# A scheduled hybrid layer kernel: context keys in the first job, later input norms, earlier input sums, fewer attention bank turns

## The chip, the cores and the metric

The kernel runs on one core of a Trainium2 chip. The metric is device time in microseconds (us) from the start to the end of one execution; a median of several executions is given. The core has five engines with their own instruction queues: TensorE (PE) multiplies and transposes, VectorE (DVE), ScalarE (ACT) and GpSimd (POOL) work elementwise, and SyncE (SP) issues the transfers here. Each engine has its instructions in one list, in the order in which they run; one whose operands aren't there waits, and those behind it with it.

## The reference, cut to what matters

One layer on 1024 latent tokens and 256 context tokens of width 1024, all in float32:

```python
mod_x = silu(c) @ w_ada + b_ada;  mod_c = silu(c_ctx) @ w_ada + b_ada     # shift, scale, gate
pl = split((rms_norm(x)   * (1 + sc_x) + sh_x) @ w_in)                      # 11 parts
pc = split((rms_norm(ctx) * (1 + sc_c) + sh_c) @ w_in)
# branch A: gated linear attention, 4 heads, key width 128, value width 256, chunks of 64, both directions
la = log_sigmoid(lowrank @ w_decay + b_decay) / 16
o_gla = forward scan + backward scan, each started from the context's final state
# branch B: differential attention, 8 heads, two score maps of width 64, value width 128
q1, q2, k1, k2 = rope(rms_norm(.) * gain);  keys: context and latent, 1280
a = softmax(q1 k1' / 8) - lam * softmax(q2 k2' / 8);  o_diff = a @ v
y = sigmoid(m_gla)  * ((rms_norm(o_gla)  * gain * silu(gla_gate))  @ w_br_gla) \
  + sigmoid(m_diff) * ((rms_norm(o_diff) * gain * silu(diff_gate)) @ w_br_diff)
return x + g_x * (y @ w_out)
```

The parts of the projection are named by what they feed: GK and GQ (keys and queries of branch A), GV, GG (its values and gate), DK, DQ, DV, DG (branch B), and MG, MD (the merge gates, "m").

## The kernel before, in words

**Precision.** A float32 product is made of three matmuls: each operand is split in a high part (ACT copies it, rounding) and a low part (DVE or POOL subtracts), and `mm3` adds high-high, low-high and high-low. So every weight tile and every activation costs a copy on ACT and a subtraction on DVE or POOL ("split") before PE can use it.

**Order.** The program is written by generators ("tasks") that run on the host while it is built. A class `Driver` keeps a clock for each engine with estimated costs, and lets that task go on whose operands are there first; so tasks of different stages interleave, and the order in which instructions are emitted is the order in each engine's queue. PE's clock is the Driver's time. `On(t, "ACT")` waits until ACT has come near t, `AtPE` until PE has, `Event` until another task has set it; `prio` breaks ties. Buffers are taken with `acq(tag)` and given back with `rel`; their numbers stand in the table `TAGS` ("w" has 16, "p" 5, "pl" 4, "e5" 6, "b1" 2). A table that ACT must load for another function has no cost in the Driver. Since every elementwise instruction is issued by one helper, all of them have line L190 in the profile, all matmuls L329, all transposes L355, all transfers L294; tiles are told apart by name.

**Stages.** (1) `prologue`: two passes of the modulation's matrix-vector product (`ada(0)`: shift and scale, `ada(1)`: the rest; PE gs, go <- w, cs and copies p<-gs), the norms of ten tiles of 128 tokens (`xnorm`: a square with its sum on ACT, a power on POOL, a multiplication on DVE), their transposes (tp <- ident, g) and the modulated, split input tiles h (`hblock`). A small job makes the low-rank decays (`prep_lr`; its la tiles are g, made by exp and log on ACT). (2) Plain projections, a list `first` of seven jobs: GK and GQ for the latent tokens, GK for the context, then dk and m by halves. A job streams its raw weights (raw), splits them (w <- raw) and walks through its items; an item is one tile of 128 output channels by up to 512 tokens, or the other way about. (3) From about 177 us branch A's scans (glab, glaf), its decayed keys and queries (ge, gqe, gqr, gkk) and their transposes and scores (gt, go, gs) run beside the later jobs. (4) From about 441 us the four large projections GV, DV, GG, DG by seven products in place of eight (`sums7`, `raws7`): sums of input blocks and of weight blocks first, s1 to s4 for the input, then the products. The sums of inputs go through p tiles; s2 overwrites input tiles h. (5) Branch A's chunks, to about 1005 us. (6) Attention: 64 units of one head and 128 queries. A unit has score banks for both maps, 1280 keys each: four banks' worth in two tiles of 128x1024, and a tail of 2 x 256 keys in one bank. `att_max` reduces a bank on DVE (sm <- s), a min joins main and tail, `att_exp` makes e with its sum on ACT, a combination of both maps follows on DVE (e <- e,sm,e), `att_tr` transposes e by groups of 4, 4 and 2 key tiles into a bank b1 for which there are two buffers, ACT copies it (ac), POOL splits it (at), and `att_av` multiplies with vv for a pair of units (b). `att_fin` normalises the pair's result (b1k), transposes it back and stores it (d_bT). Where PE has room, "fills" run: products of branch A's output with its projection (mb, mc <- h, wt), which are also what is left for behind attention. (7) The last products to 1748 us.

The parts that the change touches are these functions as they stand before:

## Time and profile before

| | |
|---|---|
| median of 3 runs | 1751.24 us (1751.02 to 1751.32) |
| the profiled execution | 1749.87 us, of which its span is 1748.2 us |
| mean granted PE clock | 0.978 of full |
| busy: PE, DVE, POOL, ACT | 1654.4, 1170.5, 951.4, 816.7 us |
| projections and branch A, 0 to 1005 us; score phase, 1004.7 to 1531.2 us | PE stands 27.0 us of the latter's 526.5 |

A row of a time line gives the start and length in us, the engine, the line, the operation, out <- in, and in square brackets how long the engine stood before it and what ended that. A row of a group gives the count, the busy time, the mean in ns and the idle time before. In a table of stretches each engine has its busy time and number of instructions; then come the granted clock, the DMA engines' busy share and GB/s. The granted clock is PE's, as a share of full.

### The profile page before, as it was taken

How to read it: one execution, taken by the hardware profiler on the slowest of the kernel's cores; microseconds unless marked ns; L12 is line 12 of the kernel's file. 1: busy time of each engine (PE TensorE's matmuls, PEld its weight loads, DVE VectorE, ACT ScalarE, POOL GpSimd, SP SyncE). 2: the span in 40 equal slices, each digit the busy share in tenths (PEclk: the TensorE clock that was granted, in tenths of full speed). 3: DMA queues.
4: the chain of work that ended last, by engine and by line, in shares of the span. 5: the costliest groups of instructions: out<-in, count | busy, mean ns of one | idle time of the engine just before them, and what ended most of it. 6: DMA issues, size and time to landing. Idle time of an engine off the chain costs nothing. (4 is left out here: it accounts for less than half of the span.)

```text
span 1748.2 us, 25274 instructions
## 1 busy us (share of the span) xinstructions
PE 1654.4 (95%) x8381; PEld 1365.3 (78%) x8381; DVE 1170.5 (67%) x1902; ACT 816.7 (47%) x1662; POOL 951.4 (54%) x1018
## 2 busy tenths in 40 slices
PE   8799799999889999999999798999999999998999
PEld 3578687888768888888888587888887788787887
DVE  4673986882844456757676568877787787735694
ACT  4675655642333334443233356565665555531241
POOL 1501775673633245655565548687788887880000
PEclk9899899999999999999999899999999999999999
DMA  8546566444225374457999823543774535368431
GB/s 301 187 151 215 165 200 202 149 135 142 84 85 161 117 253 154 160 181 250 301 297 309 225 81 102 148 123 103 216 235 129 153 103 149 94 208 296 144 105 72
DMA packets 273491, 300.82 MB, mean 172 GB/s; under 512 B 24488, under 2 KB 195408, under 8 KB 273360
## 3 DMA queue, kind: packets, MB, share of 16 engines
q1 hardware_dynamic: 273360, 299.20, 55.0%
q8 instruction: 66, 1.08, 0.3%
q14 instruction: 65, 0.53, 0.1%
HBM read 198.99 MB, written 100.14 MB: 171 GB/s over the span
## 5 line engine op out<-in xcount | busy, mean ns | idle before, releaser
L190 POOL TENSOR_TENSOR at<-ac,at 128x512 fp32r<-128x512 f32 (+1 forms) x192 | 238.1, 1240 | 16.0
L190 DVE TENSOR_REDUCE sm<-s 128x1 f32<-128x1024 f32 (+1 forms) x192 | 195.0, 1039 | 45.9 <-PE s L329 43.7
L329 PE MATMUL mm<-w,h 128*128 128x512 f32 x864 | 218.4, 402 | 4.9 <-DVE us L190 4.9
L190 ACT ACTIVATE e<-s,sm 128x1280 f32<-128x1280 f32 x128 | 169.8, 1331 | 49.6 <-DVE sm L190 41.9
L190 POOL TENSOR_SCALAR at<-ac 128x512 fp32r<-128x512 f32 (+1 forms) x192 | 141.0, 735 | 94.9 <-ACT ac L190 92.2
L329 PEld LDWEIGHTS mm<-w,h 128*128 128x128 f32 x864 | 162.4, 191 | 38.3 <-DVE us L190 5.3
L329 PE MATMUL s<-kk,aq 128*128 128x512 f32 (+1 forms) x768 | 180.7, 369 | 10.9 <-ACT e L190 6.7
L329 PE MATMUL mb<-h,wt 128*128 128x512 f32 x696 | 189.6, 405 | 0.9 <-ACT ft L190 0.7
L190 ACT ACTIVATE ac<-b 128x512 f32<-128x512 f32 (+1 forms) x212 | 106.1, 506 | 146.9 <-PE b L355 110.3
L329 PEld LDWEIGHTS s<-kk,aq 128*128 128x128 f32 x768 | 122.5, 192 | 32.8 <-ACT e L190 16.2
L329 PEld LDWEIGHTS mb<-h,wt 128*128 128x128 f32 x696 | 122.7, 189 | 22.1 <-ACT ft L190 1.1
L329 PE MATMUL mm<-h,w 128*128 128x512 f32 x552 | 137.7, 399 | 1.2 <-POOL w L190 0.6
L329 PE MATMUL b<-at,vv 128*128 128x256 f32 x960 | 129.1, 283 | 4.4 <-ACT ac L190 2.4
L190 DVE TENSOR_TENSOR w<-raw,w 128x512 fp32r<-128x512 f32 x89 | 83.3, 956 | 69.1 <-ACT w L190 49.3
L329 PEld LDWEIGHTS b<-at,vv 128*128 128x128 f32 x960 | 119.7, 188 | 10.0 <-ACT ac L190 4.4
L329 PEld LDWEIGHTS mm<-h,w 128*128 128x128 f32 x552 | 103.9, 191 | 24.2 <-DVE w L190 1.3
L190 POOL TENSOR_TENSOR w<-raw,w 128x512 fp32r<-128x512 f32 x31 | 42.8, 1382 | 136.5 <-ACT w L190 98.1
L190 DVE SCALAR_TENSOR_TENSOR e<-e,sm,e 128x1280 f32<-128x1280 f32 x64 | 113.5, 1773 | 0.7
L329 PE MATMUL mc<-h,wt 128*128 128x512 f32 x456 | 109.4, 398 | 4.4 <-DMA h<-d_bT 3.9
L190 POOL TENSOR_TENSOR sm<-sm,nhalf 128x2 f32<-128x2 f32 (+2 forms) x94 | 104.0, 1106 | 12.9 <-DVE sm L190 7.5
L329 PEld LDWEIGHTS mc<-h,wt 128*128 128x128 f32 x456 | 85.5, 190 | 24.2 <-DMA h<-d_bT 5.2
L329 PE MATMUL ma<-w,h 128*128 128x512 f32 x384 | 101.3, 404 | 0.5 <-DVE gp L190 0.4
(372 smaller groups left out, 3393.9 us busy)
## 6 DMA issues: line engine op xcount, KB each, us to landing
raw<-in_w_in SPq DMA_DIRECT2D x44, 512.0 KB, 4.7
rb<-in_w_in SPq DMA_DIRECT2D x64, 256.0 KB, 2.9
aq<-d_qT SPq DMA_DIRECT2D x128, 128.0 KB, 3.2
d_kT<-pl SPq DMA_DIRECT2D x40, 256.0 KB, 2.4
d_dv<-pl SPq DMA_DIRECT2D x40, 256.0 KB, 2.6
kk<-d_kT SPq DMA_DIRECT2D x32, 320.0 KB, 5.1
gv<-d_v SPq DMA_DIRECT2D x40, 256.0 KB, 4.6
vv<-d_dv SPq DMA_DIRECT2D x16, 640.0 KB, 6.6
```

Source lines behind the costliest of these rows:

```text
L190: self.ins = f(out, *args, **kw).ins
L329: self.ins = self.nc.tensor.matmul(out, lhsT, rhs, start=start, stop=stop, skip_group_check=more).ins
```

## The change

Four things are changed, and each moves work of several engines, since the Driver makes the whole order anew.

*Prologue.* The norms of tiles 4 to 9 wait for an event that is set when both passes of the modulation have been copied out. The low-rank job's preparation waits for the second pass's shifts and scales, no longer for the last load of the plain jobs' weights. On ACT's queue, where the modulation's copy p<-gs (4x512) stood behind a weight split of another raw tile and two squares with their sums (g to p, sm), this stands before:

```order
L190 ACTIVATE w_556<-raw_505 128x512
L190 ACTIVATE w_560<-raw_505 128x512
L190 ACTIVATE w_576<-raw_526 128x512
L190 ACTIVATE w_580<-raw_526 128x512
L190 ACTIVATE p_548,sm_549<-g_115_540 128x1024
L190 ACTIVATE p_550,sm_551<-g_116_542 128x1024
L190 ACTIVATE p_590<-gs_331 4x512
L190 ACTIVATE p_552,sm_553<-g_117_544 128x1024
```

and this now:

```order
L190 ACTIVATE w_552<-raw_509 128x512
L190 ACTIVATE w_556<-raw_509 128x512
L190 ACTIVATE p_564<-gs_335 4x512
L190 ACTIVATE p_569,sm_570<-g_115_544 128x1024
L190 ACTIVATE w_593<-raw_530 128x512
L190 ACTIVATE p_571,sm_572<-g_116_546 128x1024
L190 ACTIVATE p_609<-tp_599,shsc_197 128x512
L190 ACTIVATE w_614<-raw_530 128x512
```

The copy has moved ahead of the second raw tile's splits and of all squares.

*Keys of the context.* They are further items of the first job: GK [0, 1, 2], 12 items instead of 8 in the first job and 4 in a third. The list `first` has six jobs, four loads of raw weights and eight splits are left out. ACT's queue now has this where the GK job ends (p_1363 and p_1365 are the copies of its last, context items) and GQ's weights (w<-raw) begin; g is the decays' la:

```order
L190 ACTIVATE w_1323<-raw_577 128x512
L190 ACTIVATE w_1333<-raw_648 128x512
L190 ACTIVATE w_1343<-raw_648 128x512
L190 ACT_TABLE_LOAD
L190 ACTIVATE g_255_1191<-g_255_1191 128x1280
L190 ACTIVATE g_264_1261<-g_264_1261 128x1280
L190 ACT_TABLE_LOAD
L190 ACTIVATE g_255_1191<-g_255_1191 128x1280
L190 ACTIVATE g_264_1261<-g_264_1261 128x1280
L190 ACTIVATE p_1363<-mm_1276 128x256
L190 ACTIVATE p_1365<-ma_1277 128x256
L190 ACTIVATE w_1385<-raw_1346 128x512
```

Three more splits, from w_1291 on, stand right ahead of these rows: six of GQ's eight weight splits are ahead of the decays' two table loads, the others behind them. On PE the first transpose of branch A (gt<-ident,ge) stood right at the end of the context job; it now stands 48 matmuls into the job dk0.

*Input sums.* `sums7` no longer waits for the end of the plain projections. The sum for s2, whose place is still read by these, is stored in DRAM (four tiles of 256 KB), and after them loaded again and split into the input tiles.

*Attention.* The min is issued in `att_max`, directly behind the reductions that it joins; the task for exp then waits for ACT only. The last groups of 2 key tiles of both queries of a pair share one bank (128x512), so a pair turns the bank seven times, not nine; the e buffers of both are kept until then. `att_ot` copies a pair's result out, and `att_fin` runs once for two pairs, on 128x512. On DVE's queue one unit had this before, in the middle of attention (sm<-s is a reduction, 128x1 of a map's 1024 keys, 128x2 of the tails; sm<-sm,sm a min; e<-e,sm,e the combination of the unit before):

```order
L190 TENSOR_REDUCE sm_12442<-s_1983_9410 128x1
L190 RECIPROCAL sm_12492<-sm_12262 128x1
L190 TENSOR_SCALAR sm_12492<-sm_12492,sm_12262,nlam 128x1
L190 TENSOR_REDUCE sm_12441<-s_1983_9410 128x2
L190 TENSOR_SCALAR sm_12442<-sm_12442,sm_12441 128x1
L190 TENSOR_REDUCE sm_12443<-s_1983_9410 128x1
L190 TENSOR_TENSOR b1k_12401<-b_2678_12418,b1k_12401 128x256
L190 TENSOR_SCALAR sm_12443<-sm_12443,sm_12441 128x1
L190 SCALAR_TENSOR_TENSOR e_2681_12430<-e_2682_12431,sm_12492,e_2681_12430 128x1280
```

and has this now:

```order
L190 TENSOR_REDUCE sm_12001<-s_1967_9386 128x1
L190 TENSOR_REDUCE sm_12000<-s_1967_9386 128x2
L190 TENSOR_SCALAR sm_12001<-sm_12001,sm_12000 128x1
L190 SCALAR_TENSOR_TENSOR e_2543_12015<-e_2549_12046,sm_12064,e_2543_12015 128x1280
L190 TENSOR_REDUCE sm_12002<-s_1967_9386 128x1
L190 TENSOR_SCALAR sm_12002<-sm_12002,sm_12000 128x1
```

Nothing stands between a min and the reduction that it needs. Between the first and the last score matmul PE's list has 672 fill matmuls before and 558 now; behind the last transposes of the final norm it has 597 of their kind before and 723 now.

The diff, without the build's lists of scratch tensors and the event handling that only serves these edits:

```diff
-        e5=("sbB", 6), at4=("sbB", 6), at2=("sbB", 2), ac=("sbB", 2), b1k=("sbB", 5), fin=(None, 2),
+        e5=("sbB", 6), at4=("sbB", 6), at2=("sbB", 2), ac=("sbB", 2), b1k=("sbB", 5), ot=("sbB", 3), fin=(None, 2),
...
+            if i > 3:
+                yield ev_md
...
+            else:
+                d.set(ev_md)
...
-        first = [tra(C_GK, [0, 1], self.post_gk), tra(C_GQ, [0, 1], self.post_gq), tra(C_GK, [2], self.post_gk),
+        first = [tra(C_GK, [0, 1, 2], self.post_gk), tra(C_GQ, [0, 1], self.post_gq),
...
-        yield self.ev_plain
         for k in range(4):
             yield from self.acq("p", 4)
             v = {}
@@ -950,16 +956,27 @@
             yield d.when(v["22"])
             self.either(v["11"], v["22"], v["11"], ALU.subtract)
             yield d.when(v["11"], v["12"])
+            self.store([(self.d_s2[k], v["11"])], ev=ev_s2[k])
             self.either(v["12"], v["12"], v["11"], ALU.subtract)
-            for o, y in (("s2", "11"), ("s1", "22"), ("s4", "12"), ("s3", "21")):
+            for o, y in (("s1", "22"), ("s4", "12"), ("s3", "21")):
                 yield d.when(v[y])
-                if o != "s2":
-                    self.op7[o, k] = [self.t("s7", [P, 512], F32R) for _ in range(2)]
-                hi, lo = self.op7[o, k]
+                hi, lo = self.op7[o, k] = [self.t("s7", [P, 512], F32R) for _ in range(2)]
                 self.act.activation(hi, v[y], AF.Copy)
                 e = self.either(lo, v[y], hi.bitcast(F32), ALU.subtract)
                 d.set(self.ev_op[o, k], e)
-            self.rel("p", e, 4)
+            yield ev_s2[k]
+            self.rel("p", max(e, ev_s2[k].t), 4)
+        yield self.ev_plain
+        for k in range(4):
+            yield from self.acq("p")
+            v = self.t("p", [P, 512])
+            self.dma(v, self.d_s2[k])
+            yield d.when(v)
+            hi, lo = self.op7["s2", k]
+            self.act.activation(hi, v, AF.Copy)
+            e = self.either(lo, v, hi.bitcast(F32), ALU.subtract)
+            d.set(self.ev_op["s2", k], e)
+            self.rel("p", e)
...
-        yield self.ev_wc
+        yield self.ev_sh[1]
...
-                    d.spawn(self.att_max(u["ev"][comp], u["mx"][comp], pm, 3 * comp, 3 * comp + 1), On(e, "DVE"), prio=-3)
+                    d.spawn(self.att_max(u, comp, s5, pm, 3 * comp, 3 * comp + 1), On(e, "DVE"), prio=-3)
...
-                    d.spawn(self.att_exp(u, comp, s5), On(e, "DVE"), prio=-3)
...
-    def att_max(self, ev, mx, pm, *banks):
+    def att_max(self, u, x, s5, pm, *banks):
+
+        mx = u["mt"] if x == 2 else u["mx"][x]
         self.dve.tensor_reduce(mx, pm, AX.X, ALU.max, negate=True)
         self.banked(self.dve.ins, "DVE", *banks)
-        self.d.set(ev)
+        self.d.set(u["ev"][x])
+        for c in range(2):
+            if u["ev"][2].t is not None and u["ev"][c].t is not None and c not in u["min"]:
+                u["min"].append(c)
+                m = u["mx"][c]
+                self.dve.tensor_scalar(m, m, u["mt"][:, c:c + 1], None, ALU.min)
+                self.d.spawn(self.att_exp(u, c, s5), self.d.on("ACT", m), prio=-3)
         return
         yield
 
     def att_exp(self, u, comp, s5):
         d, mx = self.d, u["mx"][comp]
-        yield u["ev"][2]
-        yield u["ev"][comp]
-        yield d.on("DVE", mx)
-        self.dve.tensor_scalar(mx, mx, u["mt"][:, comp:comp + 1], None, ALU.min)
         yield from self.acq("e5")
         E = u["E"][comp] = self.t("e5", [P, T])
-        yield d.on("ACT", mx)
         e = self.act.activation(E, s5[:, 1280 * comp:1280 * comp + T], AF.Exp, bias=mx, accum_out=u["z"][:, comp:comp + 1])
...
+                    if n == 2 and x == 0:
+                        E0 = E
+                        continue
                     hi, lo = A[g][:2]
                     tb = "mc" if "psC" in self.pools else "b1"
                     yield from self.acq(tb)
-                    pt = self.t(tb, [P, n, P])
-                    for j in range(n):
-                        e = self.tr(pt[:, j], E[:, (k0 + j) * P:(k0 + j + 1) * P])
-                    d.spawn(self.att_split(g, pt, hi[:, :, x], lo[:, :, x], self.ev_aT[hd, qt, g], tb), On(e, "ACT"), prio=self.PS)
+                    if n == 4:
+                        pt = self.t(tb, [P, n, P])
+                        for j in range(n):
+                            e = self.tr(pt[:, j], E[:, (k0 + j) * P:(k0 + j + 1) * P])
+                        d.spawn(self.att_split(g, pt, hi[:, :, x], lo[:, :, x], [self.ev_aT[hd, qt, g]], tb), On(e, "ACT"), prio=self.PS)
+                    else:
+                        pt = self.t(tb, [P, 2, 2, P])
+                        for j in range(2):
+                            for y, EE in enumerate((E0, E)):
+                                e = self.tr(pt[:, j, y], EE[:, (k0 + j) * P:(k0 + j + 1) * P])
+                        d.spawn(self.att_split(g, pt.rearrange("p a b t -> p (a b) t"), hi.rearrange("p a b t -> p (a b) t"),
+                                               lo.rearrange("p a b t -> p (a b) t"),
+                                               [self.ev_aT[hd, qt - y, g] for y in range(2)], tb), On(e, "ACT"), prio=self.PS)
                     yield AtPE(0)
-                self.rel("e5", e)
+                if x:
+                    self.rel("e5", e, 2)
...
+                if pr % 2 == 0:
+                    yield from self.acq("fin")
...
-                d.spawn(self.att_fin(hd, pr, po, [self.att[hd, 2 * pr + x][1] for x in range(2)]), On(e, "ACT"), prio=self.PF)
+                d.spawn(self.att_ot(hd, pr, po), On(e, "ACT"), prio=self.PF)
...
+    def att_ot(self, hd, pr, po):
+
+        yield from self.acq("ot")
+        ot = self.t("ot", [P, 256])
         e = self.act.activation(ot, po, AF.Copy)
         self.rel(self.PO, e)
-        z2 = self.t("sm", [P, 2])
-        for x in range(2):
+        self.ots.append(ot)
+        if pr % 2:
+            ots, self.ots = self.ots, []
+            self.d.spawn(self.att_fin(hd, pr // 2, ots, [self.att[hd, 4 * (pr // 2) + x][1] for x in range(4)]), AtPE(e), prio=self.PF)
+
+    def att_fin(self, hd, qd, ots, zs):
+
+        d = self.d
+        yield from self.acq("b1k")
+        g = self.t("b1k", [P, 4, P])
+        self.dma(g, self.d_dg[hd // 4][qd * 512:(qd + 1) * 512, (hd % 4) * P:(hd % 4 + 1) * P].rearrange(
+            "(c p) e -> p c e", p=P))
+        z2 = self.t("sm", [P, 4])
...
+        oo = self.t("b1k", [P, 4, P])
+        ss = self.t("sm", [P, 4])
+        for x in range(4):
             e = self.act.activation(oo[:, x], pt[:, x], AF.Square, accum_out=ss[:, x:x + 1])
-        yield d.on("DVE", pt, g)
+        yield On(max(e, d.when(g)), "DVE")
         e2 = self.dve.tensor_tensor(g, pt, g, ALU.mult)
         self.rel("b1", max(e, e2))
         yield On(e, "DVE")
-        for x in range(2):
+        for x in range(4):
             self.dve.tensor_scalar(ss[:, x:x + 1], ss[:, x:x + 1], 1.0 / P, z2[:, x:x + 1], ALU.mult, ALU.add)
         yield d.on("POOL", ss)
-        yield On(self.pool.tensor_tensor(ss, ss, self.nhalf[:, 0:2], ALU.pow), "DVE")
-        for x in range(2):
+        yield On(self.pool.tensor_tensor(ss, ss, self.nhalf[:, 0:4], ALU.pow), "DVE")
+        for x in range(4):
             e = self.dve.tensor_scalar(oo[:, x], g[:, x], ss[:, x:x + 1], None, ALU.mult)
...
+        self.store([(self.d_bT[j][hd][:, qd * 512:(qd + 1) * 512], b.rearrange("p x t -> p (x t)")) for j, b in
+                    enumerate((hi, lo))], ("b1k", 2), ("fin", 1), ev=self.ev_bT[hd] if qd else None)
```

53 lines of the change are left out of this document (22 added, 31 removed).

## The prediction

> **What bounds the kernel now.** I read the page's busy shares first, then a table of stretches, then the time line at the places where TensorE (PE) stands.
>
> ```profile
> span 1748.2 us, 25274 instructions
> PE 1654.4 (95%) x8381; PEld 1365.3 (78%) x8381; DVE 1170.5 (67%) x1902; ACT 816.7 (47%) x1662; POOL 951.4 (54%) x1018
> ```
>
> PE is busy 95% of the span and no other engine is above 67%, so time can only be gained where PE stands idle (1748.2 - 1654.4 = 93.8 us by the page) or works at a lower clock. The next table (stretch, its length, busy time of PE, PE weight load, DVE, ACT and POOL, granted clock, DMA share) shows where that is.
>
> ```profile
> 25.00:50.00 25.00, 19.60 (x86) 12.14 (x85) 18.79 (x31) 15.58 (x28) 3.28 (x4) 0.93 0.87 295
> ...
> 175.00:200.00 25.00, 15.83 (x71) 12.34 (x70) 24.45 (x31) 14.49 (x45) 17.10 (x18) 0.68 0.59 193
> ...
> 400.00:450.00 50.00, 50.00 (x229) 41.52 (x229) 10.81 (x13) 13.07 (x22) 19.37 (x18) 1.00 0.40 127
> 450.00:475.00 25.00, 20.13 (x76) 16.11 (x75) 23.77 (x26) 7.63 (x14) 16.89 (x10) 0.86 0.20 64
> 475.00:500.00 25.00, 17.89 (x72) 13.90 (x71) 15.91 (x16) 9.67 (x18) 13.01 (x9) 0.86 0.24 84
> ...
> 1600.00:1748.20 148.20, 144.30 (x634) 118.67 (x632) 104.32 (x161) 36.70 (x59) 0.00 (x0) 1.00 0.37 126
> ```
>
> PE is full from 400 to 450 us, where DVE is busy for only 10.81 of 50 us; then it loses 4.87 and 7.11 us in two stretches, with DVE at 23.77 of 25 us. The starts of the program (25 to 50) and of the GLA (175 to 200) look the same. A stall also lowers the clock behind it:
>
> ```profile
> 27.00:30.40 3.40, 3.13 (x11) 2.68 (x12) 2.88 (x4) 2.80 (x6) 2.24 (x3) 0.50 0.94 311
> 50.90:61.10 10.20, 6.86 (x29) 5.74 (x30) 7.36 (x14) 6.83 (x18) 5.92 (x10) 0.50 0.64 176
> 184.00:201.00 17.00, 9.96 (x34) 7.53 (x35) 16.97 (x25) 9.66 (x34) 13.97 (x18) 0.50 0.36 110
> 467.60:474.40 6.80, 6.44 (x16) 5.09 (x17) 6.01 (x7) 0.81 (x2) 5.57 (x4) 0.52 0.22 78
> 487.80:494.60 6.80, 3.39 (x7) 2.28 (x8) 4.41 (x4) 2.79 (x5) 4.46 (x4) 0.50 0.08 29
> ...
> 1593.70:1597.00 3.30, 3.30 (x8) 2.29 (x9) 0.71 (x2) 1.06 (x1) 0.00 (x0) 0.50 1.05 382
> ```
>
> At clock 0.50 half of PE's busy time is lost too. So I price a stall as its idle time plus half of the busy time in the spell behind it: 3.4, 5.0, 3.2, 1.7 and 1.6 us for the last five rows.
>
> The Trainium skill ("TensorE: Matmul & The Clock Gate", "What's actually happening") says that about 3.4 us of idling halves the clock and about 3.4 us of sustained work restores it. The trace agrees with the unit (3.40 us at 27) but not with one busy unit being enough: at 467.6 PE works 6.44 of 6.80 us and stays at half. By the rule a stall would cost at most 1.7 us on top, and the sum below would be about 5 us smaller; I go by the rows.
>
> **A, prologue.** Norms of input tiles 4 to 9 now wait for the second modulation vector, and the low-rank job for the shifts and scales.
>
> ```profile
> 44.17 1.14 ACT L190 ACTIVATE w<-raw 128x512 fp32r<-128x512 f32 x2
> 48.26 1.15 ACT L190 ACTIVATE w<-raw 128x512 fp32r<-128x512 f32 x2 [2.96 <-DMA raw<-in_w_in]
> ...
> 51.39 0.57 ACT L190 ACTIVATE p<-gs 4x512 f32<-4x512 f32 x1
> 45.12 0.62 PE L329 MATMUL go<-pl,cs 128*2 128x512 f32 x2
> 52.02 0.58 PE L355 MATMUL gt<-ident,p 4*128 4x4 f32 x4 [6.27 <-ACT p L190]
> ...
> 57.31 1.19 PE L329 MATMUL gs<-h,pl 128*128 128x512 f32 x2 [2.04 <-DVE pl L190]
> ```
>
> The modulation's last matmul ends at 45.7, but its copy p<-gs is issued on ACT behind a weight split that waits for a transfer, and behind two squares of the norms, and runs at 51.39. In the new order it stands behind the first two splits alone: 45.8, 5.6 us sooner. The squares go behind it and are late next; but they wait for no transfer, so the first of them starts at about 46.5, where it was 49.3 (48.26 plus two splits). With the gap under 1 us the spell at 50.9 should go as well: -5.6 - 3.4 = -9.0. The 2.04 us wait may grow and cost what the spell gave; I take **-7**, ends -3 and -9.
>
> **B, keys of the context in one job.** The GK job now has 12 items and holds the context; four weight loads and eight splits go, on engines with room (DVE 67%), which I cost at nothing. What counts is that the keys are complete one query job earlier.
>
> ```profile
> 172.90 0.32 SPq L294 DMA_DIRECT2D gk<-d_k  x1
> ...
> 166.97 0.39 PE L329 MATMUL mm<-kk,w 128*128 128x256 f32 x1 [0.34 <-ACT w L190]
> ...
> 168.31 0.38 PE L329 MATMUL mm<-kk,w 128*128 128x256 f32 x1 [0.84 <-POOL w L190]
> ...
> 171.40 4.84 PE L329 MATMUL mm<-kk,w 128*128 128x256 f32 x39
> ...
> 182.87 0.44 PE L355 MATMUL gt<-ident,ge 128*128 128x128 f32 x2 [1.44 <-POOL ge L190]
> 187.35 0.69 PE L355 MATMUL gt<-ident,ge 128*128 128x128 f32 x2 [4.04 <-POOL ge L190]
> ...
> 191.65 0.69 PE L355 MATMUL gt<-ident,ge 128*128 128x128 f32 x2 [2.67 <-DVE glaf L190]
> 126.62 1.28 ACT L190 ACT_TABLE_LOAD   x1
> 127.92 2.44 ACT L190 ACTIVATE g<-g 128x1280 f32<-128x1280 f32 x2
> ```
>
> The first GLA transposes wait for ge, which is made from keys that are loaded only at 172.90, when the context job has stored them. The stall is 1.44 + 4.04 + 2.67 = 8.2 us, and 5.0 of the spell: 13.2. With the keys in the first job, 48 plain matmuls of dk0 stand ahead of the first transpose in the new order and the keys have a whole job's time: -13.
>
> The other side is the change from GK to GQ. ACT there has six weight splits, then a table load, two g, a table load, two g, and only then the splits of the query job's last two contraction tiles. That is 2 x (1.28 + 2.44) = 7.4 us in which no split is made, and the splits ahead can't run early, because their 16 buffers are given back only by the last GK group. That group is 256 wide: 4.84/39 = 0.124 us each, six per contraction tile, so 0.74 us each tile, and the six splits end about when GQ begins. A 512-wide matmul is 50.00/229 = 0.22 us by the row of 400 to 450; GQ's first group uses six tiles in 6 x 3 x 0.22 = 4.0 us and stands until the seventh, 7.4 + 0.6 + some 0.8 for two copies ahead of it, at about 8.8: a stall of 4.8, and some 2 us more at the next group's tiles, with a short spell of 2.5. **+9**; ends 0 (if the two interleaved groups use tiles half as fast, 1.36 us each) and +14. The two waits for weights inside the old context job go too (0.34 + 0.84), and I round the small waits behind 191.65 into -2. Net -13 + 9 - 2 = **-6**, ends -15 and +1.
>
> The Trainium skill ("ScalarE: Activation LUTs", "What ACT_TABLE_LOAD costs") puts a drain of 1.38 us to each load of 1.28, which would make the ACT block 10.2 us and the stall near 9. The trace shows none: the load at 126.62 ends at 127.90, and the next activation runs at 127.92.
>
> **C, input sums.** They now start without waiting for the end of the plain projections; only the s2 operand, which overwrites input tiles, is stored, loaded again and written at the end.
>
> ```profile
> 467.96 8.65 PE L329 MATMUL mm<-w,h 128*128 128x512 f32 x24 [4.87 <-DVE us L190]
> ...
> 491.08 2.15 PE L329 MATMUL gs<-w,h 128*128 128x512 f32 x3 [6.98 <-ACT h L190]
> L190 DVE TENSOR_TENSOR p<-h,h 128x512 f32<-128x512 f32 x12 | 11.7, 1019 | 2.4 <-ACT us L190 2.4
> rb<-in_w_in SPq DMA_DIRECT2D x64, 256.0 KB, 2.9
> ```
>
> The two stalls and their spells cost 4.87 + 6.98 + 3.2 + 1.7 = 16.8 us. In the new order the sums of the first two contraction tiles lie beside the last 144 matmuls of the plain projections (32 us at 0.22), where DVE was busy a fifth of the time. About half of the 48 sums and low parts, at 1.02 us, still fall behind the end, beside products that don't need them: the s2 product is third, 2 x 72 matmuls or 32 us behind. Eight transfers of 256 KB are added, 2.9 us each from issue to landing; their queue is SP's, where weight halves rb stand behind a load that waits for its store and its buffer. The DMA share there is 0.20 to 0.40, so they are covered. If the cover fails, one stall of some 3 to 9 us comes back at the first s product or at s2. **-14**, ends -8 and -17.
>
> **D, attention.**
>
> ```profile
> 1004.70:1531.20 526.50, 499.54 (x3002) 424.68 (x3001) 410.36 (x727) 311.05 (x626) 406.56 (x434) 0.99 0.48 136
> PE b L355 <- ACT ac L190: 5.8, 9, 1.0
> PE s L329 <- ACT e L190: 5.8, 9, 1.6
> 1308.66 1.54 DVE L190 SCALAR_TENSOR_TENSOR e<-e,sm,e 128x1280 f32<-128x1280 f32 x1
> 1310.12 0.21 DVE L190 TENSOR_SCALAR sm<-sm,sm 128x1 f32<-128x1 f32 x1
> ```
>
> 64 units take 526.5 us, 8.23 each; PE stands 27.0 us. The min moves ahead of a 1.54 us combination, so exp, and with it the score banks, can be 1.5 us sooner where that combination stood between. Nine bank turns per pair become seven, and the final norm runs once for four queries: fewer and wider instructions on POOL and ACT. Against that, each pair's exp buffers stay until the second query's tail, and about 114 fill matmuls (672 to 558 between the first and last score in the two orders) move behind attention: 25 us of PE work leave the phase and come back at its end, where PE is already 144.30 of 148.20 us. The phase must get 25 us shorter for nothing to change. The nearest row, DVE at 410 of 526 us, leaves room for 500 us (82%), so I take **-2**: the waits that go (some of 5.8 + 5.8) against tighter units. Ends -18 (most of 27.0 gone) and +25 (the pace stays 8.23 us a unit).
>
> **E, tail.**
>
> ```profile
> 1577.34 11.94 PE L329 MATMUL mc<-h,wt 128*128 128x512 f32 x51
> 1592.95 0.50 PE L329 MATMUL mc<-h,wt 128*128 128x512 f32 x1 [3.68 <-DMA h<-d_bT]
> ```
>
> PE waits there for a reload of the last head's output; from the last transposes to it are 11.94 + 3.68 = 15.6 us, with 51 matmuls that don't need it. In the new order 111 such matmuls stand there (24 us), so the chain is covered: -(3.68 + 1.6) = **-5**, ends 0 (some other reload is late) and -5.
>
> **Sum.** -7 - 6 - 14 - 2 - 5 = -34, against the profiled 1749.87: 1715.9. That execution is 1.4 us under the median, so a median of the changed kernel may lie as much above; it is within the rounding of the terms. I forecast **1716**.
>
> **Rivals.** (1) Chance 0.18: the stalls mostly move. GQ's missing weights take back the whole GLA gain (B 0) and the sums still end late (C -8): -7 + 0 - 8 - 2 - 5 = -22, **1728**. For it: the ACT order above, and DVE's 23.77 of 25 us; against: 32 us of product cover. (2) Chance 0.17: attention gains as well, D at -18: -50, **1700**. For it: PE waits for ac and e, which both edits shorten; against: these named waits are under 12 us. (3) Chance 0.08, the other side: attention is paced by the chain reduction, min, exp, combination, transposes, not by PE, and holding both queries' exp buffers until the second's tail, with four-query norms queued in DVE behind POOL's power, lengthens it. Each 1% of 8.23 us costs 5.3 us. With the others at -32, it decides from D = +32, that is 526.5 + 32 - 25 = 533.5 us, 1.3% over today's pace; at 3% (542 us) D is +41 and the time **1759**. For it: DVE at 78% and POOL at 77% in one dependent chain; against: POOL loses about a tenth of its work. (4) Chance 0.03: attention keeps its pace, D +25, and GQ's stall takes back the GLA gain: -7 + 0 - 14 + 25 - 5 = -1, **1749**, no difference.
>
> The forecast has 0.54. Its own range is 1706 to 1726; the one that holds eight in ten reaches into rivals 1 and 2, 1694 to 1737. Under 0.2% (3.5 us) a measurement of this kernel can't tell from no change. Faster: 0.54 + 0.18 + 0.17 = 0.89; within: 0.03; slower: 0.08.
>
> **What would show it.** A: gt<-ident,p at about 46 us, no half-clock row at 51 to 61. B: no stall at the first gt<-ident,ge, and a new one for w in the query job's first items, at about 115 to 130 us. C: no wait for us or h in the first 40 us of the products; wrong if a wait for s, h or the reload stands there. D: the score phase near 500 us; wrong if it is over 520. E: no wait for h<-d_bT. The forecast fails most likely by D, since it is the one term that is a difference of two large numbers.

## The result, and the profile after

The changed kernel takes 1724.51 us (median of 4 runs, 1722.77 to 1727.89), beside 1751.28 us of the kernel before in the same comparison: a ratio of 0.9847, 95% interval 0.9829 to 0.9864. It is 26.8 us faster; forecast were 34, and a time of 1716 with a range of 1694 to 1737. Two executions of one kernel further below (nine bank turns) were disturbed, at 2744 and 9322 us, and are left out of every figure.

The first lines of the changed kernel's page:

```profile
span 1726.2 us, 24883 instructions
PE 1646.2 (95%) x8381; PEld 1362.3 (79%) x8381; DVE 1175.0 (68%) x1876; ACT 804.2 (47%) x1606; POOL 920.9 (53%) x908
```

PE does the same 8381 matmuls and is busy for 95% of a shorter span; POOL has 110 instructions fewer and DVE as much to do as before. This profiled execution is the longest of the four (1727.89 us), so its own span is 22.0 us shorter than the profiled one of before, not 26.8.

Where these 22.0 us were won shows best by marks that both traces have: the time of a certain matmul, and how far it moved.

| mark on PE | before | after | moved by | won in this stage |
|---|---|---|---|---|
| first decay matmul (gs <- l,l) | 86.58 | 82.57 | -4.0 | -4.0 prologue (A) |
| end of the last plain projection | 441.34 | 431.25 | -10.1 | -6.1 plain jobs and branch A's start (B) |
| first score matmul | 1004.75 | 986.02 | -18.7 | -8.6 large projections (C) |
| last score matmul | 1531.57 | 1489.91 | -41.7 | -22.9 score phase |
| end | 1748.16 | 1726.17 | -22.0 | +19.7 behind it; with the line above -3.3 (D and E) |

The split between A and B is rough, because the order of the work between these marks has changed too: up to 90 us PE was busy for 76.69 us where it had been 71.19, which is 5.5 us more and not 4.0.

The table of stretches of the changed kernel, with the same columns as before:

```profile
25.00:50.00 25.00, 21.41 (x100) 13.23 (x98) 19.81 (x35) 17.38 (x31) 4.12 (x8) 0.93 0.87 291
...
175.00:200.00 25.00, 22.71 (x108) 18.09 (x107) 24.41 (x35) 14.99 (x47) 22.81 (x25) 0.93 0.56 167
...
400.00:450.00 50.00, 50.00 (x222) 41.39 (x221) 34.62 (x37) 16.39 (x29) 29.62 (x21) 1.00 0.39 124
450.00:475.00 25.00, 19.05 (x74) 15.19 (x73) 14.65 (x15) 8.89 (x16) 11.24 (x8) 0.86 0.40 133
475.00:500.00 25.00, 25.00 (x111) 20.58 (x110) 6.68 (x8) 9.94 (x18) 6.62 (x6) 1.00 0.28 88
```

At 175 to 200 PE gained 6.9 us of busy time and its clock went from 0.68 to 0.93. DVE's work of 400 to 450 us rose from 10.81 to 34.62 while PE stayed full: the input sums did move beside the last plain projection. But 450 to 475 still loses 5.95 us. Waits of PE that bear on the four parts, from its time line (in brackets: the wait in us, and what ended it):

```profile
50.16 0.66 PE L355 MATMUL tp<-ident,g 128*128 128x128 f32 x4 [1.82 <-ACT p L190]
...
131.49 0.73 PE L329 MATMUL mm<-h,w 128*128 128x512 f32 x2 [3.03 <-ACT w L190]
132.80 0.57 PE L329 MATMUL mm<-h,w 128*128 128x512 f32 x1 [0.57 <-DVE w L190]
...
458.96 8.19 PE L329 MATMUL mm<-w,h 128*128 128x512 f32 x24 [5.95 <-DVE us L190]
```

The first is the longest of those that the prologue's wait of 6.27 us left, the second and third are new, in the query job, and the fourth is the first of the two stalls of the input sums. The second of these (6.98 us for h) is gone, and so are the waits at the first gt<-ident,ge.

Two more waits lie outside the four parts:

```profile
260.16 1.11 PE L355 MATMUL tp<-ident,p 128*128 128x128 f32 x4 [3.33 <-POOL p L190]
...
982.13 1.12 PE L355 MATMUL tp<-ident,p 128*128 128x128 f32 x4 [10.32 <-POOL p L190]
```

The first is new: before, three waits of 0.87, 0.63 and 0.62 us stood in its place. The second is the longest wait of PE in the whole kernel, and it was as long before (10.33 us); nothing in the change touches it.

### The profile page after: what moved, and what is told of

It reads as the page before. It is cut to its first block, busy times and chain, and to the rows that moved or that the text cites. A ratio compares the mean times of both kernels' runs of the same rounds, so it can differ in the third digit from the quotient of the medians.

```text
span 1726.2 us, 24883 instructions
## 1 busy us (share of the span) xinstructions
PE 1646.2 (95%) x8381; PEld 1362.3 (79%) x8381; DVE 1175.0 (68%) x1876; ACT 804.2 (47%) x1606; POOL 920.9 (53%) x908
## 4 chain that ended last, share of the span: by engine, by line
PE 75%; POOL 9%; DVE 7%; issue 4%; ACT 3%; DMA 2%; SPq 0%; ACTq 0%; POOLq 0%; DVEq 0%
PE mm L329 21%; PE mc L329 10%; PE ma L329 10%; POOL at L190 6%; PE gs L329 5%; PE mb L329 5%; PE s L329 5%; PE b L329 4%; PE go L329 4%; PE gt L329 3%; PE tp L329 2%; DVE sm L190 2%; PE b L355 2%; PE tp L355 2%; DMA w<-in_w_ada 1%
## 5 line engine op out<-in xcount | busy, mean ns | idle before, releaser
L190 POOL TENSOR_TENSOR at<-ac,at 128x512 fp32r<-128x512 f32 x160 | 233.2, 1457 | 13.4
L190 ACT ACTIVATE e<-s,sm 128x1280 f32<-128x1280 f32 x128 | 169.8, 1330 | 77.1 <-DVE sm L190 63.5
L190 POOL TENSOR_SCALAR at<-ac 128x512 fp32r<-128x512 f32 x160 | 136.1, 851 | 95.2 <-ACT ac L190 90.0
L329 PE MATMUL mb<-h,wt 128*128 128x512 f32 x576 | 155.4, 404 | 4.5 <-DVE wt L190 3.1
L329 PE MATMUL mm<-h,w 128*128 128x512 f32 x576 | 149.1, 410 | 5.1 <-ACT w L190 3.2
L190 ACT ACTIVATE ac<-b 128x512 f32<-128x512 f32 x169 | 100.5, 598 | 109.8 <-PE b L355 67.4
L329 PEld LDWEIGHTS s<-kk,aq 128*128 128x128 f32 x768 | 122.5, 190 | 27.5 <-ACT e L190 10.7
L329 PE MATMUL mc<-h,wt 128*128 128x512 f32 x576 | 134.1, 393 | 0.8 <-DVE wt L190 0.5
L329 PEld LDWEIGHTS mc<-h,wt 128*128 128x128 f32 x576 | 107.5, 188 | 25.1 <-DVE wt L190 1.0
L329 PEld LDWEIGHTS mb<-h,wt 128*128 128x128 f32 x576 | 102.1, 189 | 23.7 <-DVE wt L190 4.0
L190 POOL TENSOR_TENSOR w<-raw,w 128x512 fp32r<-128x512 f32 x23 | 33.4, 1453 | 153.3 <-ACT w L190 121.5
L190 POOL TENSOR_TENSOR sm<-sm,nhalf 128x8 f32<-128x8 f32 (+3 forms) x78 | 97.7, 1252 | 10.5 <-DVE sm L190 5.3
```

The source lines that it names most:

```text
L190: self.ins = f(out, *args, **kw).ins
L329: self.ins = self.nc.tensor.matmul(out, lhsT, rhs, start=start, stop=stop, skip_group_check=more).ins
```

## The experiments

My theory was that each of the four parts acts in its own stage, on the stall named for it, and that a later stage only passes the shift on. The rival was that gains move or cancel. The experiments first undo one part each, then go into the two stalls that are left, then into attention. Each was timed beside the kernel before, on the same chip as the others of its group; the groups' medians of before lie between 1750.96 and 1752.41 us. The changed kernel was not timed again in these groups, and its own four runs lie 5.1 us apart (1722.77 to 1727.89); so a difference to its median that is under some 4 us is not shown.

### One part undone at a time

**A undone**: the changed kernel with

```diff
-            if i > 3:
-                yield ev_md
...
-        yield self.ev_sh[1]
+        yield self.ev_wc
```

> The changed kernel with the prologue as before: norms of tiles 4 to 9 wait for nothing, the low-rank preparation waits for the last plain weights again. Theory (the copy of the modulation ahead of the splits and squares is worth what the first decay matmul moved, 4.0 us, 86.6 to 82.6): the wait of about 6 us before gt<-ident,p is back, 1724.5 + 4 = about 1728.5. Rival (the prologue's gain is given back at later waits for weights): within 1.5 us of the changed kernel.

Measured 1732.70 us (1731.74 to 1733.72), ratio to before 0.9889 (0.9875 to 0.9904): 8.2 us more than the changed kernel. The prologue's waits are back, nearly as long as they were:

```profile
51.63 0.58 PE L355 MATMUL gt<-ident,p 4*128 4x4 f32 x4 [6.07 <-ACT p L190]
...
56.91 1.19 PE L329 MATMUL gs<-h,pl 128*128 128x512 f32 x2 [2.04 <-DVE pl L190]
```

The last plain projection ends at 435.55, where it was 431.25: 4.3 us of the 8.2 are in the stage, as expected; attention took 1.8 us longer in this execution, and where the other 2 us lie no mark shows. The rival, that the gain is given back, is out. The two waits of this part, the norms' and the low-rank job's, were not undone one by one.

**B undone**: the context's keys are a third job again.

```diff
-        first = [tra(C_GK, [0, 1, 2], self.post_gk), tra(C_GQ, [0, 1], self.post_gq),
+        first = [tra(C_GK, [0, 1], self.post_gk), tra(C_GQ, [0, 1], self.post_gq), tra(C_GK, [2], self.post_gk),
```

> The changed kernel with the context's keys as a third job again. Theory (the keys' early end takes away the stall at the first transposes of branch A, and the query job's missing weights give about 4 us of it back): no wait over 1 us for w in the query job, the waits of 1.4 + 4.0 + 2.7 us and their half clock back, 1724.5 + 6 = about 1730.5. Rival 1 (the query job's stall has nothing to do with the longer first job): it stays and the time is about 1737. Rival 2 (the stall was gone by other edits): about 1724.

Measured 1737.07 us (1736.11 to 1737.95), ratio 0.9914 (0.9899 to 0.9929): 12.6 us more, and 8.4 us more at the end of the last plain projection (439.62). PE's time line has the old waits back, to the hundredth:

```profile
181.01 0.44 PE L355 MATMUL gt<-ident,ge 128*128 128x128 f32 x2 [1.44 <-POOL ge L190]
185.50 0.69 PE L355 MATMUL gt<-ident,ge 128*128 128x128 f32 x2 [4.04 <-POOL ge L190]
...
189.79 0.69 PE L355 MATMUL gt<-ident,ge 128*128 128x128 f32 x2 [2.67 <-DVE glaf L190]
```

and the 3.03 us in the query job are gone (the longest wait for w in the plain jobs is now 1.05 us). So both signs of the term belong to this edit, and the net is a gain, larger than I put it.

**C undone**: the sums behind the plain projections again, with s2 written in place.

```diff
+        yield self.ev_plain
         for k in range(4):
...
-            self.store([(self.d_s2[k], v["11"])], ev=ev_s2[k])
...
-        yield self.ev_plain
-        for k in range(4):
-            yield from self.acq("p")
-            v = self.t("p", [P, 512])
-            self.dma(v, self.d_s2[k])
...
```

> The changed kernel with the sums behind the plain projections again. Theory (early sums removed the second of two stalls, 7.0 us and its half clock, and left the first, 5.95 us for us): both stalls there, 1724.5 + 8.6 = about 1733. Rival (the first stall is made anew by the store and reload of s2, and is another one than before): only the second stall's 7 us differ in place, the first is gone, time within 3 us of 1724.5.

Measured 1738.57 us (1735.72 to 1740.78), ratio 0.9922 (0.9904 to 0.9939): 14.1 us more. From the end of the plain projections to the first score it takes 564.98 us (429.02 to 994.00), against 554.77 in the changed kernel, 10.2 us more. Both stalls are there:

```profile
455.92 8.21 PE L329 MATMUL mm<-w,h 128*128 128x512 f32 x24 [5.15 <-DVE us L190]
...
478.84 2.15 PE L329 MATMUL gs<-w,h 128*128 128x512 f32 x3 [7.23 <-ACT h L190]
```

So the early sums took away the second stall and not the first, which is 0.8 us longer with them (5.95 against 5.15).

**D undone**: all of attention as before.

```diff
-    def att_max(self, u, x, s5, pm, *banks):
+    def att_max(self, ev, mx, pm, *banks):
...
-    def att_ot(self, hd, pr, po):
...
-    def att_fin(self, hd, qd, ots, zs):
+    def att_fin(self, hd, pr, po, zs):
```

> The changed kernel with attention as before: min in the exp task, nine bank turns a pair, the final norm once a pair. Theory (the score phase's 23 us are fills that moved behind attention, and only the tail's reload wait is won): score phase near 527 us against 504, the wait for h<-d_bT near 3.7 us back, time 1724.5 + 3 = about 1728. Rival (the attention edits are worth more, masked by the order of fills): 1735 or more. Other side (four-query norms cost more than they save): 1721 or less.

Measured 1730.67 us (1728.91 to 1731.51), ratio 0.9874 (0.9858 to 0.9891): 6.2 us more; 4.2 us more from the first score to the end of the profiled execution (744.39 against 740.15). The score phase is 528.3 us long again, against 503.9, with 672 fills in it, against 558, and the tail waits again:

```profile
1574.68 0.50 PE L329 MATMUL mc<-h,wt 128*128 128x512 f32 x1 [3.38 <-DMA h<-d_bT]
```

So the 23 us by which attention got shorter are nearly all work that moved behind it. The theory's 3 us were half of what it is by the medians; neither the rival's 10 nor a loss was seen.

By the medians the four parts sum to 8.2 + 12.6 + 14.1 + 6.2 = 41.1 us, more than the 26.8 of all together; by the marks of the stages they are 4.3 + 8.4 + 10.2 + 4.2 = 27.1, near the 22.0 of the profiled execution. The marks all compare with one execution of the changed kernel, the longest, 3.4 us above its median, and the sum counts this four times; by whole spans of the profiled executions the parts sum to 25.3 us. That takes up most of the difference between the two sums. But the parts' medians would sum to the whole only with a changed kernel at 1729.2 us, which is above all its runs, so part of the excess stays open.

### The query job's weights

**Decays behind the weights**: one more wait in the decays' task.

```diff
+                if (e, hh) == (1, 0):
+                    yield self.wd1[1, NK - 1]
                 for j in range(2):
                     self.act.activation(ex[j], ex[j], AF.Exp)
```

> The changed kernel with one more wait: the third pair of decays is not sent through exp and log until the query job's eight weight tiles are split, so that ACT has these splits ahead of the two table loads. Theory (the 7.4 us of decays ahead of the last two splits are the query job's whole stall): the waits for w at 128 to 135 us (4.1 us, and half the clock behind them) shrink to under 1 us and the first transpose of branch A comes 5 to 7 us earlier, near 170; time 1724.5 - 6 = about 1718. Rival (the splits are late because their buffers come free late): the waits stay above 2.5 us, time within 2 us of 1724.5.

Measured 1717.98 us (1717.28 to 1721.03), ratio 0.9817 (0.9802 to 0.9831), 6.5 us under the changed kernel. ACT's time line of this kernel:

```profile
119.36 3.75 ACT L190 ACTIVATE w<-raw 128x512 fp32r<-128x512 f32 x6
...
125.19 1.15 ACT L190 ACTIVATE w<-raw 128x512 fp32r<-128x512 f32 x2 [0.77 <-DMA raw<-in_w_in]
126.36 1.28 ACT L190 ACT_TABLE_LOAD   x1
127.65 2.43 ACT L190 ACTIVATE g<-g 128x1280 f32<-128x1280 f32 x2
```

The last two splits run at 125.19, ahead of the table loads; in the changed kernel they stood behind two table loads and four g, at 130.81 and 132.82. PE has no wait over 0.4 us in the query job; the first transpose of branch A comes at 168.61, 7.8 us earlier. The buffers were no limit: the rival is out. The 7.4 us that stood in ACT's queue were the whole stall.

### The wait for us

**Input sums on DVE alone**: in `sums7`,

```diff
-                self.either(v[o], x(0, k + dk, half).bitcast(F32), x(1, k + dk, half).bitcast(F32), ALU.add)
+                self.dve.tensor_tensor(v[o], x(0, k + dk, half).bitcast(F32), x(1, k + dk, half).bitcast(F32), ALU.add)
```

and so for the other sums and low parts there.

> The changed kernel with all sums and low parts of the input sums on DVE, none on POOL. Theory (the first stall of the large projections is left because a sum takes 1.0 to 1.8 us while both engines add and because each group of sums is handed from engine to engine four times): sums at 0.6 to 0.8 us each, the fourth group done before the products begin to need the engine, the wait for us (5.95 us) under 2 us; time 1724.5 - 7 = about 1717. Rival (DVE has simply too much to do before that point, or the groups wait for their buffers): the wait stays at 4 us or more, time within 3 us of 1724.5 or above it.

Measured 1727.18 us (1724.95 to 1729.39), ratio 0.9869 (0.9852 to 0.9885); the wait for us is 5.98 us, unchanged. The theory's forecast failed, and the time lines show why. DVE, at the start of the sums and at their fourth group, and POOL at the latter time:

```profile
400.83 2.49 DVE L190 TENSOR_TENSOR p<-h,h 128x512 f32<-128x512 f32 x4
...
439.89 6.88 DVE L190 TENSOR_TENSOR p<-h,h 128x512 f32<-128x512 f32 x4
```

```profile
420.04 1.30 POOL L190 TENSOR_TENSOR w<-ra,w 128x512 fp32r<-128x512 f32 x1 [19.59 <-ACT w L190]
...
439.50 1.63 POOL L190 TENSOR_TENSOR ra<-rb,raw 128x512 f32<-128x512 f32 x1
441.09 1.73 POOL L190 TENSOR_TENSOR raw<-raw,ra 128x512 f32<-128x512 f32 x1
```

Four sums take 2.49 us while POOL stands (for 19.59 us, to 420.04) and 6.88 us, 1.72 each, while POOL adds. Taking the input sums off POOL let the weight sums (raw, ra) go there, and the same slowing is left. It concerns additions whose operands both lie in SBUF: in the changed kernel us<-us,mm, which reads a PSUM bank, keeps its 0.67 us beside an addition on POOL, and the h<-p,h just ahead of it, with both in SBUF, takes 1.35 (the first two rows are DVE's, the third is POOL's).

```profile
458.98 1.35 DVE L190 TENSOR_TENSOR h<-p,h 128x512 fp32r<-128x512 f32 x1
460.26 0.67 DVE L190 TENSOR_TENSOR us<-us,mm 128x512 f32<-128x512 f32 x1
...
459.74 1.72 POOL L190 TENSOR_TENSOR h<-p,h 128x512 fp32r<-128x512 f32 x1
```

The Trainium skill ("GPSIMD Engine Reference", "1. Specifications") says that POOL shares its SBUF interfaces with VectorE, with contention where DVE reads two inputs from SBUF; these rows agree, with a factor of 2.8 in the first pair (6.88 to 2.49 us).

**Weight sums held back**: in the weight sums of the third product, and where us is added,

```diff
+                            if g == 0 and k == 2:
+                                yield self.ev_us1
...
+                    if n == 1 and t == 1 and g == 0:
+                        d.set(self.ev_us1)
```

> The changed kernel with the weight sums of the third product's last two contraction tiles held back until the second copy of us is issued. Theory (the 5.95 us are work that stands in DVE's queue ahead of us<-us,mm without being needed before it, at 1.7 us an instruction while POOL adds too): the wait for us falls from 5.95 to 2 to 3 us, as the three instructions of 4 us leave the place ahead of it, and the products need no weight later; time 1724.5 - 4 = about 1720.5, 1719 if the half clock goes with it. Rival (the weights held back are then missed by the third product): the wait moves there, for w, and the time stays at 1723 to 1727.

Measured 1724.41 us (1723.76 to 1725.12), ratio 0.9843 (0.9822 to 0.9863): 0.1 us less than the changed kernel, where 4 were expected. PE's time line and DVE's:

```profile
456.71 7.37 PE L329 MATMUL mm<-w,h 128*128 128x512 f32 x24 [3.53 <-DVE us L190]
```

```profile
447.17 4.11 DVE L190 TENSOR_TENSOR p<-p,p 128x512 f32<-128x512 f32 x4
451.98 0.69 DVE L190 TENSOR_TENSOR s<-p,s 128x512 fp32r<-128x512 f32 x1 [0.70 <-ACT s L190]
453.02 3.04 DVE L190 TENSOR_TENSOR w<-ra,w 128x512 fp32r<-128x512 f32 x2 [0.35 <-ACT w L190]
455.98 0.68 DVE L190 TENSOR_TENSOR us<-us,mm 128x512 f32<-128x512 f32 x1
```

In the changed kernel this stood in DVE's queue at the same place:

```profile
453.68 1.75 DVE L190 TENSOR_TENSOR raw<-raw,ra 128x512 f32<-128x512 f32 x1
455.36 1.75 DVE L190 TENSOR_TENSOR w<-ra,w 128x512 fp32r<-128x512 f32 x1
...
458.23 0.67 DVE L190 TENSOR_TENSOR us<-us,mm 128x512 f32<-128x512 f32 x1
```

The wait fell from 5.95 to 3.53 us, and no wait for w came in its place; the stage from the plain projections' end to the first score is 551.8 us, 3.0 us shorter. So 2.4 us of the stall are made by weight sums that stand ahead of us<-us,mm in DVE's queue and aren't needed before it. The rest is argued from the rows and not tested: the fourth group's input sums and two w<-ra of 1.5 us each still stand ahead of it, and DVE waits 0.70 and 0.35 us for ACT among them. The profiled execution is 3.1 us shorter than the changed kernel's; the ratio is the same within its interval, so on the whole time 3 us are not shown.

### Attention's three edits

**The min alone undone**: the min goes back into `att_exp`.

```diff
     def att_exp(self, u, comp, s5):
         d, mx = self.d, u["mx"][comp]
+        yield u["ev"][2]
+        yield u["ev"][comp]
+        yield d.on("DVE", mx)
+        self.dve.tensor_scalar(mx, mx, u["mt"][:, comp:comp + 1], None, ALU.min)
         yield from self.acq("e5")
         E = u["E"][comp] = self.t("e5", [P, T])
+        yield d.on("ACT", mx)
```

> The changed kernel with the min back in the task for exp. Theory (attention's 6.2 us are the tail's reload and a little of each edit): score phase 1 to 3 us longer than 504, exp waiting longer for the min on DVE than now, time 1725 to 1728. Rival (the min is what keeps the denser phase at PE's pace): score phase 10 us or more longer, or as many fills fewer behind it, time over 1730.

Measured 1718.17 us (1717.10 to 1719.12), ratio 0.9814 (0.9800 to 0.9829): 6.3 us *less*. Neither side had this. The score phase is 507.1 us, 3.2 more than in the changed kernel, but holds 594 fills and not 558, and from the first score to the end it takes 733.3 us against 740.2. The waits of PE in the score phase, of the changed kernel and of this one (in all, times, longest):

```profile
PE b L355 <- ACT ac L190: 8.8, 13, 1.3
PE s L329 <- ACT e L190: 6.1, 11, 1.5
PE b L329 <- ACT ac L190: 5.7, 6, 1.2
```

```profile
PE s L329 <- ACT e L190: 8.8, 11, 1.9
...
PE b L355 <- ACT ac L190: 2.4, 3, 1.3
PE b L329 <- ACT ac L190: 1.4, 3, 0.8
```

With the early min PE waits 2.7 us less for exp and 10.7 us more for ac, the copies of the transposed banks. In all it stands 30.8 us in the score phase, against 23.6 with the min undone. These 7.2 us are about the 6.8 by which this run is shorter from the first score to the end. That the exps, placed earlier in ACT's queue, hold the copies up would fit; but ACT doesn't stand longer for the min with the early min (63.5 us against 70.8 in this stretch), so that is not shown.

**The shared bank alone undone**: nine bank turns again.

```diff
-                    if n == 2 and x == 0:
-                        E0 = E
-                        continue
...
-                        pt = self.t(tb, [P, 2, 2, P])
...
-                if x:
-                    self.rel("e5", e, 2)
+                self.rel("e5", e)
```

> The changed kernel with nine bank turns a pair, each query's tail group in a bank of its own. Theory (POOL and the two b1 banks had slack; fewer turns bring little): time 1724 to 1728, waits b<-ac on PE as now within 3 us. Rival (the bank turns are the attention edit that counts): PE waits for ac 5 us and more longer in the score phase, time 1730 or more.

Two executions took 1719.24 and 1721.76 us, ratio 0.9828 (0.9808 to 0.9847), some 4 us less than the changed kernel. There is no profile of either, so only the times are used: the rival, 1730 or more, is out. That the shared bank by itself costs time is not shown, because two executions stand against four and the intervals overlap; nor does it show a gain here.

**The four-query norm alone undone**:

```diff
-    def att_ot(self, hd, pr, po):
...
-    def att_fin(self, hd, qd, ots, zs):
+    def att_fin(self, hd, pr, po, zs):
```

> The changed kernel with the final norm once a pair, as before; min and bank turns stay changed. Theory (taken alone, going back on the min gained 6.3 us and going back on all three cost 6.2, so the four-query norm must be what attention gains by): time 1730 or more, DVE's waits for POOL's power in the score phase longer. Rival (the three edits only shift which fills the order leaves for behind attention): within 4 us of 1724.5.

Measured 1728.05 us (1725.25 to 1728.92), ratio 0.9861 (0.9843 to 0.9880): 3.5 us more, with an interval that overlaps the changed kernel's (0.9829 to 0.9864), so a loss is not shown. It lies within the rival's bound and under the theory's 1730. The score phase takes 516.3 us and holds 615 fills: as the rival has it, other fills are left for behind attention.

**The four-query norm alone kept**: min and shared bank undone together.

> The changed kernel whose attention has only the four-query norm: min in the exp task, nine bank turns. Theory (min and the shared bank each cost some 4 to 6 us in this order): faster than either undone alone, 1712 to 1717, with more fills than 594 inside the score phase at under 515 us. Rival (either edit alone already frees what there is, or they need each other): 1718 to 1725.

Measured 1734.31 us (1731.29 to 1735.34), ratio 0.9897 (0.9878 to 0.9916): 9.8 us more than the changed kernel, where 7 to 12 less were expected. Nearly all fills (696) stand inside the score phase, which takes 528.8 us, and nothing is left to cover the end:

```profile
1577.77 12.46 PE L329 MATMUL mc<-h,wt 128*128 128x512 f32 x41 [8.19 <-DMA h<-d_bT]
```

So the three don't add. Undone, the min gains 6.3 us and the bank loses nothing, but together they lose 9.8. What goes with the time is the order that comes of it: with 594 fills in the phase and the tail covered it is fastest, with 696 the last reload stands open for 8.19 us. From the first score to the end PE stands 28.1 us with the min undone, 37.1 in the changed kernel and 41.1 here. Which instruction in the order decides the rest is open.

### What helps, together

The changed kernel with the decays' wait, the weight sums' wait, and the min back in `att_exp` (the three diffs above).

> The changed kernel with the three things that helped: the third pair of decays behind the query job's weights, the weight sums of two contraction tiles behind the second us, and the min back in the task for exp. Theory (the three lie in stages that only pass a shift of start on to each other, so they add): 6.5 + 3 + 6.3 = 15.8 us less than the changed kernel, 1709, with no wait over 1 us for w in the query job, about 3.5 us for us and 594 fills in the score phase. Rival (the gains are one execution's order and don't add): 1714 to 1718.

Measured 1707.72 us (1705.58 to 1707.82), ratio 0.9746 (0.9731 to 0.9762): 16.8 us less than the changed kernel, 43.2 less than before. PE's waits of the two stalls:

```profile
447.04 8.47 PE L329 MATMUL mm<-w,h 128*128 128x512 f32 x24 [3.55 <-DVE us L190]
```

and in the plain jobs up to 170 us it has no wait for w over 0.4 us. The marks add: the first transpose of branch A at 168.24 (168.61 with the first wait alone), the sums' stage 552.9 us (551.8), the first score to the end 731.5 us (733.3). The theory's 1709 is met, so these gains, which lie in different stages, add; those of attention's edits don't.

## Why the prediction was right, step by step

The sign holds, the time lies in the range, and each of the five terms lies within its ends or next to them. But only B and E came as put. A, C and D were all too hopeful, by 3.0, 5.4 and 4.0 us, and that is the 12 us between the 34 forecast and the 22.0 of the profiled execution. By the medians the forecast was 8.5 us too low. That the time is in the range is owed to the range, 43 us wide, as well as to the terms.

| term | forecast | by the marks | what differed |
|---|---|---|---|
| A, prologue | -7 | -4.0 | the spell of half clock stayed |
| B, keys | -6 | -6.1 | the new stall smaller, the net as put |
| C, sums | -14 | -8.6 | the first stall stayed, at 5.95 |
| D, attention | -2 | +2.0 | PE stands longer, not shorter |
| E, tail | -5 | -5.3 | the wait and its spell are gone |

(The marks give D and E together, -3.3: 22.9 us less score phase and 19.7 us more behind it. For E the price of before's wait, 3.68 + 1.6, is put, and the rest is D's.)

**A.** The copy of the modulation runs at 45.20, the forecast 45.8, and the wait of 6.27 us is gone. What failed is "with the gap under 1 us the spell at 50.9 should go as well". PE waits 0.67, 1.82, 0.53 and 0.39 us between 46 and 54, for norms, copies and h that come late one after another, and the clock still halves, as this stretch of the changed kernel shows (the second row is the query job's spell, of which B speaks):

```profile
51.10:57.90 6.80, 6.16 (x16) 4.69 (x17) 6.35 (x10) 5.26 (x15) 4.57 (x7) 0.50 0.79 235
133.00:139.80 6.80, 6.28 (x15) 4.23 (x15) 6.13 (x9) 3.88 (x7) 0.00 (x0) 0.51 0.73 253
```

Half of 6.16 us is 3.1 us, so of the 3.4 us put on the spell only 0.3 were won; and where PE stood 6.27 + 0.19 + 2.04 = 8.5 us, it still stands 3.4.

The prediction also misread how long a spell lasts, where it says that one busy unit is not enough at 467.6. The spells last whole units of 3.41 us (the rows that it shows are one, two, three and five of them long), and cut along these, the row at 467.6 falls in two; the third row is the unit ahead of the changed kernel's spell at 51.16:

```profile
467.32:470.73 3.41, 2.77 (x7) 2.21 (x8) 3.41 (x4) 1.09 (x3) 3.41 (x3) 0.50 0.20 77
470.73:474.15 3.42, 3.42 (x10) 2.68 (x9) 2.88 (x4) 0.00 (x0) 2.19 (x2) 0.50 0.22 78
...
47.75:51.16 3.41, 1.25 (x10) 0.77 (x8) 2.06 (x4) 3.39 (x6) 1.46 (x3) 1.00 0.97 346
```

In the first unit PE is busy for 2.77 us only, the second it fills, and behind that one the clock is back. One filled unit was enough here; the spell is longer because the unit in which the work starts again wasn't filled. In the third row no wait is over 1.82 us, but they leave PE 1.25 us of work in one unit.

**B.** Both mechanisms came as put, in their places: no wait at the first transpose, and the new stall for w at 128 to 135 us. It was 3.03 + 0.57 + 0.16 + 0.36 = 4.1 us and a spell of 6.8 us with 6.28 us of work in it (3.1), 7.2 us in all, beside the +9 of the working, where the first stall was put at 4.8 us. Undoing the edit costs 8.4 us net by the mark, and mending the new stall alone gains 6.5 us by the medians; so the early keys alone are worth some 15 us, as the working has it (13 and 2), and the new stall 6.5 to 7.2, where it has 9.

**C.** Half of it. The second stall and its spell were priced at 6.98 + 1.7 = 8.7 us, and 8.6 were won by the marks; the first was to go too, and it stayed: the sign set for this, no wait for us, did not come. "About half of the sums still fall behind the end, beside products that don't need them" is the step that failed. The half is right (23 of 48 start behind it), and the products don't need the sums. But they need DVE, to empty a PSUM bank by us<-us,mm, and that stands in DVE's queue behind sums of inputs and of weights. The stall is not a matter of s2's reload, whose lower end I had in mind; it is there without the early sums too (5.15 us). The sums were also dearer than the 1.02 us that the prediction took from the row of the group: over 1.7 us while POOL adds, which that mean hides. Two rows of the kernel before that are in it:

```profile
441.06 1.29 DVE L190 TENSOR_TENSOR p<-h,h 128x512 f32<-128x512 f32 x2
...
456.09 5.18 DVE L190 TENSOR_TENSOR p<-h,h 128x512 f32<-128x512 f32 x3
```

That is 0.65 us a sum in the first and 1.73 in the second.

**D and E.** 25 us of fills left the phase and came back behind it, as put, and the last reload is covered: behind the last transposes (to 1531.5) PE runs on for 26 us, and the first wait behind these is 0.23 us, for wt.

```profile
1531.22 26.36 PE L329 MATMUL mc<-h,wt 128*128 128x512 f32 x114
1557.81 0.74 PE L329 MATMUL mc<-h,wt 128*128 128x512 f32 x2 [0.23 <-ACT wt L190]
```

That attention took 2 us more and not 2 less goes back to the step "the waits that go (some of 5.8 + 5.8)": they didn't go. The score phase of the changed kernel:

```profile
986.00:1489.90 503.90, 473.05 (x2912) 406.39 (x2911) 412.70 (x706) 304.53 (x584) 386.28 (x338) 1.00 0.46 132
```

It is 22.6 us shorter than before with 26.5 us less of work for PE, so PE stands 30.9 us there and not 27.0: the waits of b<-ident,e for ac rose from 5.8 to 8.8 us, and those for e from 5.8 to 6.1. This is one order's result: the four orders with part of these edits gave between 6.3 us less and 9.8 us more than it, by the medians.

**The rivals.** The first (stalls move, 1728) is nearest to the time, and half of it happened, in C; the second (attention gains as well) did not; the third (attention paced by its chain and slower) did not, as the phase took 503.9 us and the point of decision was 533.5; nor did the fourth, no difference.

## What to carry to other kernels

Instructions that are moved out of a stall still stand in an ordered queue: before moving work "beside something that doesn't need it", list what the other engine still has to get from the same queue there, down to the one that frees a bank. An order made from estimated costs goes wrong where a cost is missing, so look for table loads and for two engines adding at once, and place the urgent instruction by a wait rather than by an estimate. Measure edits of different stages apart, by marks of their own stage, since whole times of one kernel spread by several us; edits of the same loop have to be tried in each combination.

## What the runs showed of the hardware

- An addition of 128x512 on DVE with both operands in SBUF takes 0.62 us while POOL is idle and 1.72 us while POOL adds such tiles too; one that reads a PSUM bank keeps its 0.67 us. Taking some of these additions off POOL brought nothing, because others took their place there.
- Short waits of PE halve the clock too: for 6.8 us from 51.16 on, behind a unit of 3.41 us in which PE was busy for 1.25 us with no wait over 1.82. The spell ended behind the first unit that PE filled (3.42 us of work from 54.57 to 57.99; in the unit ahead of it 2.83).
- Two table loads and their four activations hold ACT for 7.4 us; the two splits of 0.6 us that stood behind them cost PE 4.1 us and half its clock for 6.8.
